# A two-layer decoder trunk on one core: accounts of written work for the scalar engine, the vector engine and SP

## The chip, the core and the metric

The kernel runs on one of the eight cores of one Trainium2 chip. The core has a tensor engine (PE, whose weight loads are shown as PEld), a vector engine (DVE), a scalar engine (ACT), GpSimd (POOL) and a sync engine (SP), which here does nothing but issue DMAs. Each engine works through its own instructions in order; semaphores hold an instruction back until its operands are there. The metric is the device time of one execution in microseconds (us), as the median of several runs. One execution more is profiled, and its trace is read below.

## The reference

Two layers on x of 512 x 2048 in float32. Each layer makes a modulated RMS norm, a branch and a gated residual add:

```python
for i in range(DEPTH):
    shift, scale, gate = jnp.split(c_act @ w_mod[i] + b_mod[i], 3, axis=-1)
    h = rms_norm(x, norm_w[i]) * (1.0 + scale) + shift
    out = fox_branch(h, ...) if i == 0 else rwkv7_branch(h, v_first, ...)
    x = x + gate * out
```

Layer 0 is a forgetting attention with 32 heads of 64. Layer 1, which the change is about, is RWKV-7 time mixing:

```python
r, k, v, z = xr @ w_in[0], xk @ w_in[1], xv @ w_in[2], xg @ w_in[3]   # x*: shifted mixes of h
kk = k * k_k;  kk = kk / max(norm(kk per head), 1e-12)
k = k * (1.0 + (a - 1.0) * k_a)
def step(S, inp):                       # 512 steps, S of 64 x 64 for each head
    S = S * w_t + (S @ a_t) b_t^T + v_t k_t^T        # a = -kk, b = kk * a
    return S, S @ r_t
y = group_norm(y) * lnx_w + lnx_b + sum(r * k * r_k) * v
return (y * silu(z)) @ w_out
```

## The kernel before

Activations are kept transposed, as 16 tiles of 128 channels by 512 tokens. Every projection is made in three passes of float32r products (weight high half x high half, low x high, high x low), so that each k step of a projection tile is three matmuls of 128x512 (`mm3`; the groups named pj<-hi,whi and so on). A weight tile of four k steps (256 KB) comes in by a DMA on SP (raw), ACT rounds it (whi, `act_hi`), and DVE subtracts (wlo). Layer 1 has 10 + 64 such tiles in one row: the rest of k, then r, v, z and at last the output projection (wo).

These projections are the **backbone** (`backbone`, L319). All else of layer 1 is done by **tasks**: Python generators that write instructions and then `yield` a distance in planned microseconds. A planned clock, `Flow.t`, goes on with each matmul that is written, by its size alone (L91 to 96). Before each k step the backbone lets every task go on whose due time has come. So the order in which instructions are written is set by those distances, and this is the order in which ACT, DVE and PE carry them out (`InOrder` chains them, and all their instructions have line L90). Where a projection's weights or operands are not written yet, the planned clock is put on by 0.2. Nothing in the plan knows how much work was already given to ACT, DVE or SP.

The tasks that the change touches, in the order of time:

- `keys` (L1305), one for each of the 16 tiles of k, started every KEY = 9.8 planned us: three loads (ip, kt, aa), a square (sq), exponentials (eI, eN), the mean of the squares by a product with a block matrix in a bank S, then kk, at, bk, their stores (atd, bkd), small products (gab) and their stores (mld). `means` (L1097) splits the square in two halves, mhi by ACT and mlo by DVE, and multiplies both into S. `mixz` makes the shifted mix for z beside it. Every four keys an inversion of small triangles is made (`invert` on POOL, for the last group on DVE; `inverse` for the products).
- `stage` (L1475), one for each of 16 units (four key tiles, two chunks of 64 tokens): loads of rt, bk, prk, then decays, and the operands of the chunk products (`products`). `bonus` makes the added term, again with `means`.
- `recur` writes the 32 steps of the recurrence, each in three hops of 3.9 planned us. `normed` (L1640) makes the group norm of a unit: two `means`, a reciprocal root, and the store ypd<-dc.
- `gated` (L1692): a tile of z goes through Silu into one of two z buffers, which frees its projection bank; when its group's ypd is complete it is loaded (yp, one buffer), multiplied (z<-z,yp) and stored (gd<-z). The output projection reads it back (hp<-gd) and splits it. The projection bank of a tile is that of the tile two before.

## Time and profile before

| | |
|---|---|
| median of 3 runs | 2400.13 us (2396.8 to 2401.81) |
| profiled execution, its own time | 2401.73 us |
| its span, first to last instruction | 2399.9 us |
| mean granted PE clock | 0.982 |
| busy share: PE, PEld, DVE, ACT, POOL | 96%, 75%, 67%, 52%, 29% |
| DMA | 480.23 MB, 200 GB/s on average |

Layer 1's backbone starts near 1179 us. The key stage runs from about 1350 to 1680 us, the recurrence to about 2190 us, and the output projection ends with the span. A row of a stage table gives the window, its length, then busy time and number of instructions of PE, PEld, DVE, ACT and POOL, the granted PE clock, the DMA share and GB/s. A row of waits says which engine and tile waited for whom, the microseconds in total, how often, and the longest. A row of a timeline has start and duration, the instruction, and in brackets the idle time of its engine just before it with what ended it.

### The profile page before, as it was taken

How to read it: one execution, taken by the hardware profiler on the slowest of the kernel's cores; microseconds unless marked ns; L12 is line 12 of the kernel's file. 1: busy time of each engine (PE TensorE's matmuls, PEld its weight loads, DVE VectorE, ACT ScalarE, POOL GpSimd, SP SyncE). 2: the span in 40 equal slices, each digit the busy share in tenths (PEclk: the TensorE clock that was granted, in tenths of full speed). 3: DMA queues.
4: the chain of work that ended last, by engine and by line, in shares of the span. 5: the costliest groups of instructions: out<-in, count | busy, mean ns of one | idle time of the engine just before them, and what ended most of it. 6: DMA issues, size and time to landing. Idle time of an engine off the chain costs nothing. (4 is left out here: it accounts for less than half of the span.)

```text
span 2399.9 us, 39413 instructions
## 1 busy us (share of the span) xinstructions
PE 2302.2 (96%) x13626; PEld 1807.3 (75%) x13626; DVE 1605.2 (67%) x2850; ACT 1256.5 (52%) x2300; POOL 694.4 (29%) x1114
## 2 busy tenths in 40 slices
PE   6999999999999999998999898899999899999999
PEld 4787777877778778886777676677777677777787
DVE  6886778888888635336797567666476776755322
ACT  4435655555565545225646777763345556665221
POOL 0002333442424210110141208771245535450000
PEclk8999999999999999999999999899999999999999
DMA  8864466766666346445756999886867766544543
GB/s 307 328 227 156 128 211 217 222 213 213 205 224 220 114 161 225 142 141 157 223 179 198 308 263 277 256 252 187 233 187 195 219 174 194 167 132 154 161 137 97
DMA packets 388152, 480.23 MB, mean 200 GB/s; under 512 B 146032, under 2 KB 217840, under 8 KB 384112
## 3 DMA queue, kind: packets, MB, share of 16 engines
q1 hardware_dynamic: 386288, 475.08, 63.7%
q0 software_dynamic: 1664, 2.63, 0.3%
q8 instruction: 108, 1.77, 0.3%
q14 instruction: 92, 0.75, 0.1%
HBM read 381.63 MB, written 95.95 MB: 199 GB/s over the span
## 5 line engine op out<-in xcount | busy, mean ns | idle before, releaser
L90 PE MATMUL pj<-hi,whi 128*128 128x512 f32 x2416 | 987.4, 409 | 11.0 <-ACT hi L90 8.2
L90 PE MATMUL pj<-hi,wlo 128*128 128x512 f32 x2416 | 959.4, 397 | 10.1 <-DVE wlo L90 10.0
L90 PE MATMUL pj<-lo,whi 128*128 128x512 f32 x2416 | 959.9, 397 | 0.0
L90 DVE TENSOR_TENSOR wlo<-raw,whi 128x512 fp32r<-128x512 f32 (+2 forms) x628 | 473.4, 761 | 255.1 <-ACT whi L90 252.4
L90 ACT ACTIVATE whi<-raw 128x512 fp32r<-128x512 f32 (+2 forms) x628 | 393.9, 634 | 399.0 <-PE pj L90 215.1
L90 PEld LDWEIGHTS pj<-hi,whi 128*128 128x128 f32 x2416 | 459.5, 190 | 116.8 <-ACT hi L90 9.2
L90 PEld LDWEIGHTS pj<-lo,whi 128*128 128x128 f32 x2416 | 458.3, 190 | 108.4 <-DVE lo L90 0.7
L90 PEld LDWEIGHTS pj<-hi,wlo 128*128 128x128 f32 x2416 | 459.9, 190 | 105.2 <-DVE wlo L90 13.4
L90 DVE CUSTOM_DVE_ANT_0 wm<-wm,cb 128x1024 f32<-128x1024 f32 x128 | 155.8, 1217 | 0.3
L90 POOL TENSOR_SCALAR SV<-SV,dec 64x64 f32<-64x64 f32 x224 | 94.2, 442 | 103.9 <-DVE SV L90 69.7
L90 ACT ACTIVATE pr<-Sm,mx 128x128 f32<-128x128 f32 (+3 forms) x128 | 71.5, 559 | 76.8 <-POOL mx L90 76.3
L90 POOL TENSOR_SCALAR pr<-pr,rc 128x128 f32<-128x128 f32 (+3 forms) x128 | 100.8, 788 | 26.0 <-DVE rc L90 23.6
L90 POOL TENSOR_SCALAR mx<-mx 128x1 f32<-128x1 f32 x128 | 59.9, 468 | 143.2 <-DVE mx L90 98.0
L90 DVE CUSTOM_DVE_ANT_0 Sm<-S,cmask 128x128 f32<-128x128 f32 (+3 forms) x128 | 62.3, 487 | 42.5 <-PE S L90 41.8
L90 POOL TENSOR_TENSOR lt<-lane 128x30 f32<-128x30 f32 (+14 forms) x90 | 64.2, 713 | 86.4 <-DMA lane<-mld 79.6
L90 POOL TENSOR_TENSOR bk<-bk,eI 128x512 f32<-128x512 f32 x32 | 36.6, 1142 | 110.3 <-PE S L90 64.0
L90 POOL TENSOR_TENSOR lane<-lane,lt 128x30 f32<-128x30 f32 (+14 forms) x90 | 64.0, 711 | 7.0
L90 PE MATMUL S<-k,q 128*128 128x128 f32 (+7 forms) x256 | 61.9, 323 | 0.0
L90 POOL TENSOR_TENSOR acc<-acc,sq 128x512 f32<-128x512 f32 x14 | 18.1, 1296 | 149.4 <-ACT sq L90 128.2
L90 ACT ACTIVATE pT<-tr 128x512 f32<-128x512 f32 x64 | 31.0, 485 | 54.4 <-PE tr L90 54.4
L90 DVE SCALAR_TENSOR_TENSOR hp<-pj,gate,hp 128x512 f32<-128x512 f32 x16 | 12.0, 751 | 68.0 <-PE pj L90 68.0
L90 PE MATMUL tr<-ident,pr 128*128 128x128 f32 x320 | 56.0, 273 | 1.5 <-DVE pT L90 1.3
(325 smaller groups left out, 3284.0 us busy)
## 6 DMA issues: line engine op xcount, KB each, us to landing
wm<-in_wmodT SPq DMA_DIRECT2D x132, 512.0 KB, 4.4
raw<-in_wz SPq DMA_DIRECT2D x128, 256.0 KB, 3.7
raw<-in_wo SPq DMA_DIRECT2D x128, 256.0 KB, 3.6
raw<-in_wv SPq DMA_DIRECT2D x124, 256.0 KB, 3.9
wm<-in_wmodT SPq DMA_DIRECT2D x30, 1024.0 KB, 6.4
raw<-in_wk SPq DMA_DIRECT2D x96, 256.0 KB, 3.7
raw<-in_wr SPq DMA_DIRECT2D x64, 256.0 KB, 5.0
raw<-in_wq SPq DMA_DIRECT2D x56, 256.0 KB, 3.5
```

The costliest lines, as they stand in the source:

```text
L90: self.last = f(*a, **k)
```

## The change

`InOrder` gets an account: `until` is the planned time at which all that was written for this engine will be done, with 0.38 for a DMA issue and 0.08 + 0.0008 for each element of a partition for other instructions (0.49 for 512). `room(left)` lets a task wait in steps of 0.2 until no more than `left` (0.6, for SP 0.8) stands open. Accounts are kept in layer 1 for ACT, DVE and SP; the backbone's own weight loads and splits are booked but do not wait, and nor do `mixing`, `mixed`, `inverse` (but for its loads), `recur`, `products`, `values` and the loads of `gathering`. The tasks above wait for room at the places that the diff shows, and at these places that are cut from it: sp.room(0.8) ahead of the stores mld<-gab and qtd<-qt and of the loads qt<-qld; in `normed` act.room() ahead of dc and of the reciprocal root, dve.room() ahead of each of the eight dc products, sp.room(0.8) ahead of ypd<-dc; dve.room() ahead of bonus's product. Some of their own distances become shorter: 8 to 6, 2.2 to 1.4 and 2 to 1.2 in `keys`; 1 to 0.4, 0.6 to nothing, 0.6 to 0.2 and 2 to 0.6 in `stage`.

```diff
     def __init__(self, tc, engine):
         self.tc, self.engine, self.on, self.last, self.clock = tc, engine, False, None, None
+        self.flow, self.until = None, 0
...
+            if self.flow and "table" not in name:
+                n = 1
+                for d in (k.get("out", a[0] if a else None)).shape[1:]:
+                    n *= d
+                self.until = max(self.until, self.flow.t) + (
+                    0.38 if name == "dma_start" else 0.08 + n * 8e-4)
             return self.last
         return issue
+
+    def room(self, left=0.6):
+
+        while self.until - self.flow.t > left:
+            yield 0.2
...
     def means(q, w, x, th, tl):
         hi = q.tile([P, T], R, tag=th, name="mhi")
         lo = q.tile([P, T], R, tag=tl, name="mlo")
+        yield from act.room()
         act_hi(hi, x)
...
         m = q.tile([P, T], F, tag="mm", name="m", bufs=2)
+        yield from act.room()
         act.activation(m, hp[:, 1:], AF.Copy, scale=omu[:, 2, k:k + 1])
         yield 1.5
+        yield from dve.room()
...
         yield 1.5
+        yield from sp.room(0.8)
         sp.dma_start(mxd[2, k], m)
...
     def keys(q, j):
         ip = q.tile([P, T], F, tag="ip", name="ip", bufs=2)
         sp.dma_start(u3(ip), of(ipd, j))
+        yield from sp.room(0.8)
         kt = load(q, kTd[j], "kt", bufs=2)
+        yield from sp.room(0.8)
         aa = load(q, aad[j], "aa", bufs=2)
-        yield 8
+        yield 6
         sq = q.tile([P, T], F, tag="sq", name="sq")
+        yield from act.room()
         act.activation(sq, kt, AF.Square, scale=col(V_KK, j))
         yield from take("eI")
         eI = eIs[0]
+        yield from act.room()
         act.activation(eI[:, :, 1:], c3(ip), AF.Exp, scale=-EDEC)
-        yield 2.2
+        yield 1.4
         ss, n = yield from means(q, blkr, sq, "mh", "ml")
...
         yield from take("eN")
+        yield from act.room()
         eN = q.tile([P, NCH, C], F, tag="eN", name="eN")
         act.activation(eN, c3(ip), AF.Exp, scale=EDEC)
-        yield 2
+        yield 1.2
...
         yield 0.7
+        yield from act.room()
         act.activation(aa, aa, AF.Identity, scale=col(V_KA, j), bias=oka[:, j:j + 1])
...
         for i in range(2):
+            yield from sp.room(0.8)
             sp.dma_start(bkd[j // NJ][:, :, i, j % NJ], ...)
...
     def stage(q, g, u):
...
-        yield 1
+        yield 0.4
         for i in range(2):
             for h in range(2):
+                yield from sp.room(0.8)
                 sp.dma_start(bk.rearrange("p j c i t -> p (j c) i t")[HS[h], :, i, :],
                              bkd[g][HS[h], u, i ^ h].rearrange("p j (c t) -> p (j c) t", c=UC))
-            yield 0.6
         yield from take("prk")
...
         yield STW
         eI = q.tile([P, NJ, UC, C], F, tag="eI", name="eI", bufs=2)
+        yield from act.room()
         act.activation(eI, prk, AF.Exp, scale=-EDEC)
         yield 1
+        yield from dve.room()
...
         for j in range(NJ):
+            yield from dve.room()
...
                 s, t = HS[h], OS[h]
+                yield from dve.room()
                 sp.dma_start(L[h][s, :, 0, :], atd[g][s, u, :, c * C:c * C + C])
...
+                yield from sp.room(0.8)
                 sp.dma_start(SV[h][t], vtd[g][(UC * u + c) * C:(UC * u + c + 1) * C, h])
...
-                yield 0.6
+                yield 0.2
             fl.start(fl.t + STW, products(q, m, c, L, SV, qp, bk, eI, dec))
-            yield 2
+            yield 0.6
...
     def bonus(q, g, u, prk):
+        yield from sp.room(0.8)
...
         sp.dma_start(u3(yp), of(ypd, j))
-        yield 4
-        yield 1
+        yield 5
+        yield from dve.room()
         dve.tensor_tensor(out=z, in0=z, in1=yp, op=OP.mult)
...
-    pe.clock = fl
+    pe.clock = act.flow = dve.flow = sp.flow = fl
```

Added lines in the class move the common line of all instructions from L90 to L91. Three places in the order of instructions follow, first before the change and then with it.

ACT in the key stage, at the fifth key: sq, eI and aa belong to it or the key before it, whi is the backbone's next weight tile, m is the mix for z, r a finished tile of r, and t the first use of the mean product.

```order
L90 ACTIVATE sq<-kt,vecs 128x512
L90 ACTIVATE eI<-ip 128x8x64
L90 ACTIVATE aa<-aa,oka,vecs 128x512
L90 ACTIVATE whi<-raw 128x512
L90 ACTIVATE m<-hp,omu 128x512
L90 ACTIVATE mhi<-sq 128x512
L90 ACTIVATE whi<-raw 128x512
L90 ACTIVATE t<-S,nfloor 128x512
```

```order
L91 ACTIVATE sq<-kt,vecs 128x512
L91 ACTIVATE eI<-ip 128x8x64
L91 ACTIVATE whi<-raw 128x512
L91 ACTIVATE aa<-aa,oka,vecs 128x512
L91 ACTIVATE mhi<-sq 128x512
L91 ACTIVATE r<-pj 128x512
L91 ACTIVATE m<-hp,omu 128x512
L91 ACTIVATE whi<-raw 128x512
L91 ACTIVATE t<-S,nfloor 128x512
```

The mix m has gone from ahead of mhi to behind it; three instructions stand between sq and mhi where four stood.

SP in the unit stage, at the loads of the tenth unit: rt, the four loads of bk and prk are the unit's, vv is its bonus's, raw is a weight tile of z.

```order
L90 DMA rt<-rTd 128x512
L90 DMA SV_20200<-vtd 64x256
L90 DMA SV_20201<-vtd 64x256
L90 DMA vvd<-vf 512x1x128
L90 DMA raw<-in_wz 128x512
L90 DMA bk<-bkd 64x8x64 x4
L90 DMA prk<-ipd 128x512
L90 DMA vv<-vvd 128x512
```

```order
L91 DMA rt<-rTd 128x512
L91 DMA raw<-in_wz 128x512
L91 DMA bk<-bkd 64x8x64 x3
L91 DMA raw<-in_wz 128x512
L91 DMA bk<-bkd 64x8x64
L91 DMA prk<-ipd 128x512
L91 DMA vv<-vvd 128x512
```

The loads of bk no longer stand in one piece; a weight load has come between them.

ACT where the output projection begins: z<-pj is the Silu of a z tile (the last two of them are tiles 14 and 15), hi<-hp and hi<-z split the output projection's operands, whi is a weight tile.

```order
L90 ACTIVATE hi<-hp 128x512 x3
L90 ACT_TABLE_LOAD
L90 ACTIVATE z<-pj 128x512
L90 ACTIVATE whi<-raw 128x512
L90 ACTIVATE hi<-hp 128x512 x2
L90 ACTIVATE whi<-raw 128x512
L90 ACTIVATE z<-pj 128x512
L90 ACTIVATE whi<-raw 128x512
L90 ACTIVATE hi<-z 128x512
```

```order
L91 ACTIVATE hi<-hp 128x512 x3
L91 ACTIVATE whi<-raw 128x512 x2
L91 ACT_TABLE_LOAD
L91 ACTIVATE z<-pj 128x512 x2
L91 ACTIVATE whi<-raw 128x512
L91 ACTIVATE hi<-hp 128x512 x2
L91 ACTIVATE whi<-raw 128x512
L91 ACTIVATE hi<-z 128x512 x2
```

The two last Silus now stand one behind the other, ahead of the weight tile and the two splits that stood between them.

More of the change, by code (lines that the diff above doesn't have):

```diff
@@ L1520, in stage @@
                                            4 * h + u, :].rearrange("j p t -> p j t"))
+                yield from sp.room(0.8)
                 sp.dma_start(SV[h][t], vtd[g][(UC * u + c) * C:(UC * u + c + 1) * C, h])
@@ L1569, in bonus @@
     def bonus(q, g, u, prk):
+        yield from sp.room(0.8)
         vv = q.tile([P, T], F, tag="vv", name="vv", bufs=1)
@@ L1659, in normed @@
         act.activation(sq, d, AF.Square)
+        yield from act.room()
         act.activation(dc, d, AF.Copy)
@@ L1668, in normed @@
             act.preload_act_table_set("natural_log_exp_and_others")
+        yield from act.room()
         r = rstd_of(q, vr, lneps, 64e-5, "sq", False, bufs=2)
@@ L1672, in normed @@
         for j in range(NJ):
+            yield from dve.room()
             s = slice(j * P, (j + 1) * P)
@@ L1676, in normed @@
         for j in range(NJ):
+            yield from dve.room()
             s = slice(j * P, (j + 1) * P)
@@ L1681, in normed @@
         yield 1.8
+        yield from sp.room(0.8)
         sp.dma_start(ypd[g][:, u], dc.rearrange("p (j t) -> p j t", j=NJ))
@@ L1704, in gated @@
         sp.dma_start(u3(yp), of(ypd, j))
-        yield 4
-        yield 1
+        yield 5
+        yield from dve.room()
         dve.tensor_tensor(out=z, in0=z, in1=yp, op=OP.mult)
```

1 line of the change is left out of this document (added).

## The prediction

> **What bounds the kernel now.** I read the page first, then busy time by stage, then what TensorE (PE) waited for in each stage, then what the engine that released it had waited for.
>
> ```profile
> span 2399.9 us, 39413 instructions
> PE 2302.2 (96%) x13626; PEld 1807.3 (75%) x13626; DVE 1605.2 (67%) x2850; ACT 1256.5 (52%) x2300; POOL 694.4 (29%) x1114
> ```
>
> PE is busy for 96% of the span, so it sets the end, and a change of order can win only PE's idle time and the time in which its clock is halved. Next the stages of layer 1's main part (time, busy time of each engine, granted clock, DMA share): the key stage, the unit stage with the recurrence, the change-over to the output projection, and the output projection.
>
> ```profile
> 1350.00:1680.00 330.00, 300.89 (x2189) 233.45 (x2188) 222.62 (x324) 213.65 (x398) 162.63 (x220) 0.93 0.86 251
> 1680.00:2190.00 510.00, 492.96 (x4696) 386.74 (x4695) 339.61 (x721) 279.44 (x485) 219.87 (x423) 0.99 0.65 182
> 2190.00:2229.00 39.00, 36.01 (x151) 27.72 (x150) 22.98 (x42) 21.93 (x35) 0.00 (x0) 1.00 0.68 215
> 2229.00:2397.00 168.00, 167.04 (x719) 135.11 (x717) 48.91 (x73) 36.03 (x57) 0.00 (x0) 1.00 0.42 129
> ```
>
> PE is idle for 29.1 us in the key stage, 17.0 in the unit stage, 3.0 in the change-over and 1.0 after it. The last row also gives PE's pace when nothing holds it: 168 / 719 = 0.234 us a matmul, 0.70 us for the three of one k step. What ended PE's waits, key stage first, then unit stage, then change-over:
>
> ```profile
> PE S L90 <- ACT mhi L90: 10.5, 5, 3.9
> PE S L90 <- DVE mlo L90: 8.4, 9, 2.0
> PE pj L90 <- DVE wlo L90: 7.1, 3, 2.8
> PE x L90 <- ACT us L90: 2.9, 4, 1.0
> ...
> PE S L90 <- ACT GP L90: 9.7, 5, 5.3
> PE S L90 <- ACT mhi L90: 3.5, 1, 3.5
> ...
> PE pj L90 <- DVE wlo L90: 2.9, 3, 1.5
> ```
>
> In the key stage 18.9 of 28.9 us is the wait of the small mean product in bank S for its operand's two halves, mhi from ACT and mlo from DVE, which `means` makes. The longest of these waits, on ACT and then on PE:
>
> ```profile
> 1554.22 0.63 ACT L90 ACTIVATE whi<-raw 128x512 fp32r<-128x512 f32 x1 [4.26 <-DMA raw<-in_wr]
> 1554.87 1.16 ACT L90 ACTIVATE qt<-x 32x256 f32<-32x256 f32 x3
> 1556.06 0.72 ACT L90 ACTIVATE sq<-kt,vecs 128x512 f32<-128x512 f32 x1
> ...
> 1558.43 0.71 ACT L90 ACTIVATE m<-hp,omu 128x512 f32<-128x512 f32 x1
> 1559.04 0.61 ACT L90 ACTIVATE mhi<-sq 128x512 fp32r<-128x512 f32 x1
> ...
> 1559.71 0.80 PE L90 MATMUL S<-mhi,blkr 128*128 128x512 f32 x1 [3.91 <-ACT mhi L90]
> ```
>
> ACT works in order. It stood 4.26 us for a weight tile that came late, and then worked off what was queued; four instructions, among them m, stood between sq and mhi (m to mhi took 0.61 us). So two things make PE late: late weight DMAs, which no account sees, and the queue ahead of mhi, which the accounts do see. The first is the larger part:
>
> ```profile
> ACT whi L90 <- DMA raw<-in_wr: 33.6, 20, 4.8
> ACT whi L90 <- DMA raw<-in_wv: 7.4, 2, 4.0
> ...
> ACT eI L90 <- DMA prk<-ipd: 7.5, 4, 4.1
> ```
>
> The first two rows are the key stage's, 41.0 us on ACT; the third is the unit stage's. Each longer wait of PE also costs clock. Windows around four mhi or mlo waits, then two of the unit stage:
>
> ```profile
> 1365.00:1380.00 15.00, 9.84 (x33) 7.34 (x32) 10.48 (x13) 13.33 (x24) 4.64 (x4) 0.77 0.88 278
> 1440.00:1455.00 15.00, 12.20 (x51) 9.03 (x50) 8.00 (x11) 10.42 (x19) 10.41 (x18) 0.77 0.98 306
> 1495.00:1505.00 10.00, 8.40 (x40) 5.85 (x39) 7.19 (x11) 7.21 (x13) 8.88 (x16) 0.83 1.07 332
> 1555.00:1567.00 12.00, 7.41 (x34) 4.95 (x33) 7.57 (x10) 9.04 (x17) 10.12 (x17) 0.72 1.04 328
> ...
> 1735.00:1745.00 10.00, 7.76 (x66) 6.08 (x68) 6.47 (x16) 4.09 (x7) 0.00 (x0) 0.83 0.72 205
> 1912.00:1925.00 13.00, 7.72 (x82) 5.80 (x82) 8.42 (x16) 7.70 (x15) 6.22 (x16) 0.74 0.85 246
> ```
>
> Length times missing clock gives 3.5 + 3.5 + 1.7 + 3.4 = 12.1 us for the four and 1.7 + 3.4 = 5.1 us for the two.
>
> **The key tasks: act.room() and sp.room().** They remove nothing and add no work; instructions change places. In the order of ACT's instructions 57 stand between the sixteen sq and their mhi before, 40 now: one fewer a key, or 0.6 us earlier by m's 0.61 us, while the planned distance from mhi to PE's product is as before. The places of SP's DMAs help less: a weight load has 4.1 others ahead of it on average both before and now, and runs of seven or more fall from nine to five. That is why I let the late DMAs stand. Taking 0.6 us off each of 5 + 9 waits gives 3.0 + 5.0 (nine of 0.93 us on average, each left with about 0.4) = 8 us. Clock falls in proportion: 8 / 18.9 of 12.1 = 5 us. Sum **−13 us**. The bounds: 0, if late DMAs set all of these waits, and −31 us, if none of them is left (18.9 + 12.1). I take the nearer to the low end because of the 41.0 us above. The waits for wlo (7.1 us) and us (2.9 us) stay. The first come where group 3's inversion runs on DVE, which stood
>
> ```profile
> 1605.52 0.19 DVE L90 TENSOR_TENSOR lt<-lane 128x30 f32<-128x30 f32 x1 [10.04 <-DMA lane<-mld]
> ```
>
> for a load that its task asks for with no distance in between; `invert` is not touched.
>
> The shorter own distances (8 to 6, 2.2 to 1.4, 2 to 1.2) I cost at nothing: the room waits ahead of them fill them up again, and the planned start of every key is the old one. Without that cover a key's three loads would be asked for about 2 us later than they are wanted, at most once a key and hidden by PE's queue of projection matmuls, until ACT stands for them; that possibility goes into the range.
>
> The Trainium skill ("TensorE: Matmul & The Clock Gate", section "Part 1: The HAM clock gate (the "warmup" mystery)") says that the clock halves after an idle window of about 3.4 us. The window at 1440 above has 2.8 us of idle in two pieces and a clock of 0.77, so here shorter waits halve it as well, and the measurement decides. By the Trainium skill's rule alone only the two longest spells would cost clock, 6.9 us instead of 12.1, and the sum would be 2 us smaller.
>
> **The unit tasks: stage, bonus, normed.** PE's 9.7 + 3.5 us come when ACT stands for prk (7.5 us) or for a weight, and the copies that free bank S stand behind it. The loads of bk ahead of prk on SP now wait for room, so prk is asked for nearer to its planned time; a weight load now stands among the four. I take a third: 13.2 / 3 = 4.4, and 0.6 of clock: **−5 us**. Bounds: 0, and −18 us (13.2 + 5.1).
>
> **The change-over pays.** The waits push the recurrence back against the projections. After the last variance product (S<-mlo,blkr) PE has 858 projection matmuls left before and 822 now; the last 768 are the output's. So the output's first tile starts 90 x 0.234 = 21.1 us after it before, and 54 x 0.234 = 12.6 us now: 8.4 us of cover is gone. What has to happen between, as it ran before:
>
> ```profile
> 2192.96 0.69 ACT L90 ACTIVATE sq<-S,lneps 128x512 f32<-128x512 f32 x1
> 2197.69 0.33 SPq L90 DMA_DIRECT2D ypd<-dc  x1
> 2199.92 0.52 SPq L90 DMA_DIRECT2D yp<-ypd  x1
> 2204.45 0.69 DVE L90 TENSOR_TENSOR z<-z,yp 128x512 f32<-128x512 f32 x1 [1.14 <-DMA yp<-ypd]
> 2205.17 0.52 SPq L90 DMA_DIRECT2D yp<-ypd  x1
> 2206.41 1.36 SPq L90 DMA_DIRECT2D gd<-z  x1
> 2208.99 0.69 DVE L90 TENSOR_TENSOR z<-z,yp 128x512 f32<-128x512 f32 x1 [3.85 <-DMA yp<-ypd]
> 2211.68 0.60 ACT L90 ACTIVATE z<-pj 128x512 f32<-128x512 f32 x1
> ```
>
> The Silu of tile 14 frees the bank of the output's first tile, and it writes the z buffer that the store of tile 12 (gd<-z) reads. Counted from the first row, that store is issued at +13.5; with 2.2 us to land (the store of ypd, 2197.69, to the load that waits for it, 2199.92) and 0.6 for the Silu the bank is free at +16.3. Before, this was 4.8 us early; now it is 3.7 us late. The Silu of tile 15 stands right behind on ACT and waits for the second product (+16.0), which is 0.4 us later than its own tile wants; the weight halves that queue behind these two cost an estimated 1.5 us, the length of the longest wlo wait here. A PE wait of that length cost 3.4 us of clock at 1555. The 2.9 us of wlo waits there now go under. 3.7 + 0.4 + 1.5 + 3.4 − 2.9 = **+6 us**. Bounds: 0 if the bank comes in time, and +12 (8.4 + 3.4).
>
> **Sum.** The profiled execution took 2401.73 us, 1.6 above the median of the runs: 2401.7 − 13 − 5 + 6 = 2389.7, and at the median **2388 us**. Its own range, with half and one and a half of the gain of 18 and the cost between 3 and 9: 2376 to 2400.
>
> **Rivals.** First, **nothing to gain**: the key stage is held by the DMA engines, whose share is 0.86 on average and 0.98 to 1.07 in three of the four windows above, so the weights come late in any order. Against it: the window at 1365 has 0.88, and the average leaves 14%. Then 0 to −6 us there and in the units against +6: 2400. The Trainium skill ("DMA: Bandwidth & Descriptors", section "Specifications") asks for 512 B or more in a transfer for line rate; that speaks for this rival and is a limit that order does not move. The row
>
> ```profile
> DMA packets 110265, 82.68 MB, mean 251 GB/s; under 512 B 41531, under 2 KB 84027, under 8 KB 110233
> ```
>
> of this stage shows 38% of packets below that. By that rule alone the time would stay at 2400.
>
> Second, **slower by the change-over**: the chain above is serial over one yp buffer, ACT stands in order with both Silus ahead of the weights, and so the whole 8.4 us comes back as PE idle, with 3.4 of clock; where the gain upstream is under 4 us, the time is above 2405, at 2409 with none (2400.1 + 8.4 + 3.4 − 2.9). It decides as soon as the store of tile 12 lands after the last projection of tile 15. Against it: part of the 8.4 us was slack (4.8 us).
>
> Third, **most S waits vanish**: half a microsecond was often all that lacked (mean mlo wait 0.93 us), and one avoided wait spares the clock for the next key. Three quarters of 31 + 18 against +6: 2401.7 − 37 + 6 − 1.6 = 2369.
>
> **Chances.** Forecast 0.42, nothing to gain 0.20, slower by the change-over 0.22, most S waits vanish 0.16. What a measurement here can tell from no change is about 0.2%, 4.8 us: faster means under 2395.3. Of the forecast's 0.42 I count 0.38 there and 0.04 as the same; of the first rival 0.03 falls below. Faster 0.57, same 0.21, slower 0.22. Cases of both signs count, so the range for 8 in 10 goes from the third rival to the second: 2367 to 2408.
>
> **What would show it.** Right: PE's mhi and mlo waits in the key stage fall from 18.9 to about 11 us while ACT's waits for raw stay near 41; PE's waits for GP fall in the unit stage; a new wait of pj for ACT z, near 4 us, stands at the start of the output projection. Wrong: raw waits fall as well (then SP's places matter more than I count, and the third rival is near); no wait for ACT z (the change-over was covered); new ACT waits for kt or aa (the short distances were too short); or mhi waits as long as before with the clock again at 0.93.

## The result, and the profile after

| | before | after |
|---|---|---|
| median | 2400.97 us (2396.8 to 2408.12, 4 runs) | 2425.3 us (2423.27 to 2429.01, 4 runs) |
| ratio, 95% interval | | 1.0099, 1.0083 to 1.0116 |
| profiled execution's span | 2399.9 us | 2424.3 us |

The change makes the kernel 1.0% slower, 24 us. The prediction was 2388 us, faster; sign and range were both wrong. First the page of after:

```profile
span 2424.3 us, 39413 instructions
PE 2313.8 (95%) x13626; PEld 1814.1 (75%) x13626; DVE 1614.3 (67%) x2850; ACT 1261.3 (52%) x2303; POOL 700.4 (29%) x1114
```

PE's work is the same, ACT has three table loads more (35 for 32), and PE is still the engine that sets the end. Next the stage tables of both kernels, this time cut at events instead of fixed times, so that they can be compared: layer 1's backbone up to the first unit, the unit stage with the recurrence up to the last variance product, and the change-over with the output projection. Before:

```profile
1179.00:1709.00 530.00, 493.74 (x3120) 381.01 (x3119) 368.69 (x504) 326.80 (x601) 211.39 (x270) 0.96 0.80 239
1709.00:2192.00 483.00, 465.96 (x4458) 364.84 (x4457) 329.47 (x704) 269.90 (x466) 215.11 (x406) 0.99 0.64 177
2192.00:2400.00 208.00, 201.05 (x860) 161.22 (x858) 70.89 (x113) 56.51 (x90) 0.00 (x0) 1.00 0.47 145
```

After:

```profile
1182.00:1719.00 537.00, 497.39 (x3145) 383.74 (x3144) 367.60 (x506) 326.61 (x601) 211.71 (x270) 0.97 0.80 238
1719.00:2219.00 500.00, 475.55 (x4468) 369.82 (x4467) 343.93 (x710) 279.57 (x476) 219.31 (x406) 0.98 0.62 172
2219.00:2424.00 205.00, 194.78 (x825) 156.74 (x823) 66.37 (x106) 51.86 (x82) 0.00 (x0) 0.98 0.46 140
```

Projection matmuls move between the stages with the order, so a stage's length isn't its loss. What can be compared is PE's idle time (the exact length less PE's busy time) plus the clock it lost (half of the time for which the trace's clock records give half speed). The change-over is counted to PE's last matmul. "Key stage" is the first row. "Cover" is the number of projection matmuls that PE still has ahead of the output projection when the last variance product is done:

| us idle + lost clock | layer 0 | key stage | unit stage | change-over and output | cover (matmuls) | median us |
|---|---|---|---|---|---|---|
| before | 52.9 | 58.5 | 22.1 | 3.0 | 90 | 2401 |
| after | 53.1 | 55.0 | 34.6 | 11.6 | 54 | 2425 |
| difference | +0.2 | −3.5 | **+12.5** | **+8.6** | | +24 |

The sum is 17.8 us of 24.4. Of the rest, 2.7 us lie in layer 0, where PE's order is the same in both kernels; across the profiles below layer 0 took between 1177.0 and 1184.2 us. So a few us in one profile carry nothing. The measure of the table scatters too: in layer 0, where the order is one in all the profiles below, it runs from 47.3 to 56.9 us, and e4 below, whose order is that of the kernel before until 1700 us, has 53.2 us in its key stage for 58.5. The remaining 4 us I can't place.

PE's waits after, first in the key stage (1350 to 1680 us):

```profile
PE S L91 <- DVE mlo L91: 9.7, 10, 3.0
PE S L91 <- ACT mhi L91: 9.5, 8, 2.0
PE pj L91 <- DVE wlo L91: 8.7, 3, 5.0
PE S L91 <- ACT gab L91: 2.6, 1, 2.6
```

mhi and mlo together are 19.2 us, 18.9 before: nothing was won. In the unit stage (1680 to 2190 us), before (the rows that the prediction doesn't show) and after:

```profile
PE S L90 <- DVE mlo L90: 1.8, 4, 0.6
...
PE S L90 <- DVE vf L90: 0.3, 1, 0.3
```

```profile
PE S L91 <- ACT GP L91: 6.7, 4, 3.4
PE S L91 <- DVE mlo L91: 5.6, 7, 2.2
PE S L91 <- ACT mhi L91: 3.2, 1, 3.2
PE S L91 <- ACT sq L91: 2.5, 2, 1.4
PE S L91 <- POOL SV L91: 1.7, 1, 1.7
PE S L91 <- DVE vf L91: 1.7, 1, 1.7
```

The waits for prk, from which the prediction started here, went as it said:

```profile
ACT eI L91 <- DMA prk<-ipd: 1.6, 2, 0.9
```

They took 7.5 us before. GP fell from 9.7 to 6.7 us, but mlo rose from 1.8 to 5.6 and vf from 0.3 to 1.7, and sq and POOL's SV are new. What ACT itself waited for in the key stage:

```profile
ACT whi L91 <- DMA raw<-in_wr: 40.8, 23, 4.8
...
ACT whi L91 <- DMA raw<-in_wv: 7.2, 5, 2.2
```

and, before and then after, in the unit stage:

```profile
ACT whi L90 <- DMA raw<-in_wv: 23.8, 13, 5.2
```

```profile
ACT whi L91 <- DMA raw<-in_wv: 31.7, 11, 5.7
```

ACT's waits for late weights rose from 41.0 to 48.0 and from 23.8 to 31.7 us. Why a shorter queue ahead of mhi did not shorten PE's waits is seen at a key of after, on ACT, PE and DVE:

```profile
1508.28 0.63 ACT L91 ACTIVATE whi<-raw 128x512 fp32r<-128x512 f32 x1 [4.36 <-DMA raw<-in_wr]
1508.82 0.71 ACT L91 ACTIVATE sq<-kt,vecs 128x512 f32<-128x512 f32 x1
...
1510.65 0.61 ACT L91 ACTIVATE mhi<-sq 128x512 fp32r<-128x512 f32 x1
...
1511.32 0.50 PE L91 MATMUL S<-mhi,blkr 128*128 128x512 f32 x1 [1.51 <-ACT mhi L91]
...
1512.39 1.06 DVE L91 TENSOR_TENSOR mlo<-sq,mhi 128x512 fp32r<-128x512 f32 x1
...
1513.51 0.50 PE L91 MATMUL S<-mlo,blkr 128*128 128x512 f32 x1 [1.69 <-DVE mlo L91]
```

ACT stood 4.36 us for a weight tile ahead of sq, and though only eI and aa stand between sq and mhi, PE still waited. All five of PE's mhi waits before (10.5 us) have such a stall of ACT, 1.8 to 4.3 us long, ahead of sq. Of the eight after the change (9.5 us), three (5.4 us) are of this kind; three (1.8 us) have a weight stall of 1.5 to 2.2 us between sq and mhi; and in two (2.3 us) ACT stood there 2.1 and 2.7 us with eI, for DVE to write at. Over the sixteen keys ACT ran 57 instructions between sq and mhi before and 40 after, nine of them whi in both; the idle time ahead of those nine rose from 1.5 to 11.0 us, and the mean time from the start of sq to that of mhi from 2.91 to 3.21 us.

At the change-over, on ACT and then on PE:

```profile
2220.78 0.69 ACT L91 ACTIVATE sq<-S,lneps 128x512 f32<-128x512 f32 x1
...
2236.61 1.28 ACT L91 ACT_TABLE_LOAD   x1 [5.63 <-DVE z L91]
2237.90 0.60 ACT L91 ACTIVATE z<-pj 128x512 f32<-128x512 f32 x1
...
2238.55 0.80 PE L91 MATMUL pj<-hi,whi 128*128 128x512 f32 x1 [6.45 <-ACT z L91]
```

```profile
2230.00:2245.00 15.00, 8.55 (x25) 6.45 (x25) 3.67 (x6) 4.83 (x8) 0.00 (x0) 0.66 0.71 218
```

The predicted new wait is there, 6.45 us long, with 15 x 0.34 = 5.1 us of clock behind it.

### The profile page after: what moved, and what is told of

Read it like the earlier page. It is cut to its first block, busy times and chain, and to the rows that moved or that the text cites. A ratio compares the mean times of both kernels' runs of the same rounds, so it can differ in the third digit from the quotient of the medians.

```text
span 2424.3 us, 39413 instructions
## 1 busy us (share of the span) xinstructions
PE 2313.8 (95%) x13626; PEld 1814.1 (75%) x13626; DVE 1614.3 (67%) x2850; ACT 1261.3 (52%) x2303; POOL 700.4 (29%) x1114
## 5 line engine op out<-in xcount | busy, mean ns | idle before, releaser
L91 PE MATMUL pj<-hi,whi 128*128 128x512 f32 x2416 | 991.9, 411 | 17.8 <-ACT hi L91 8.2
L91 PE MATMUL pj<-hi,wlo 128*128 128x512 f32 x2416 | 962.4, 398 | 8.7 <-DVE wlo L91 8.7
L91 PE MATMUL pj<-lo,whi 128*128 128x512 f32 x2416 | 962.5, 398 | 0.0
L91 DVE TENSOR_TENSOR wlo<-raw,whi 128x512 fp32r<-128x512 f32 (+2 forms) x628 | 467.8, 752 | 273.1 <-ACT whi L91 270.6
L91 ACT ACTIVATE whi<-raw 128x512 fp32r<-128x512 f32 (+2 forms) x628 | 394.2, 634 | 415.9 <-PE pj L91 231.8
L91 PEld LDWEIGHTS pj<-hi,whi 128*128 128x128 f32 x2416 | 461.5, 191 | 124.5 <-ACT hi L91 9.0
L91 PEld LDWEIGHTS pj<-lo,whi 128*128 128x128 f32 x2416 | 460.3, 191 | 109.1 <-DVE lo L91 0.2
L91 PEld LDWEIGHTS pj<-hi,wlo 128*128 128x128 f32 x2416 | 462.0, 191 | 102.9 <-DVE wlo L91 10.7
L91 DVE CUSTOM_DVE_ANT_0 wm<-wm,cb 128x1024 f32<-128x1024 f32 x128 | 155.7, 1216 | 0.3
L91 POOL TENSOR_SCALAR SV<-SV,dec 64x64 f32<-64x64 f32 x224 | 94.3, 443 | 90.8 <-DVE SV L91 77.6
L91 ACT ACTIVATE pr<-Sm,mx 128x128 f32<-128x128 f32 (+3 forms) x128 | 71.5, 559 | 77.0 <-POOL mx L91 76.4
L91 POOL TENSOR_SCALAR pr<-pr,rc 128x128 f32<-128x128 f32 (+3 forms) x128 | 101.3, 791 | 25.8 <-DVE rc L91 23.6
L91 POOL TENSOR_SCALAR mx<-mx 128x1 f32<-128x1 f32 x128 | 60.0, 469 | 145.3 <-DVE mx L91 100.3
L91 DVE CUSTOM_DVE_ANT_0 Sm<-S,cmask 128x128 f32<-128x128 f32 (+3 forms) x128 | 62.2, 486 | 42.5 <-PE S L91 41.9
L91 POOL TENSOR_TENSOR lt<-lane 128x30 f32<-128x30 f32 (+14 forms) x90 | 62.5, 695 | 84.6 <-DMA lane<-mld 77.7
L91 POOL TENSOR_TENSOR bk<-bk,eI 128x512 f32<-128x512 f32 x32 | 38.0, 1189 | 125.3 <-PE S L91 73.3
L91 POOL TENSOR_TENSOR lane<-lane,lt 128x30 f32<-128x30 f32 (+14 forms) x90 | 65.3, 725 | 7.1
L91 PE MATMUL S<-k,q 128*128 128x128 f32 (+7 forms) x256 | 61.9, 323 | 0.0
L91 POOL TENSOR_TENSOR acc<-acc,sq 128x512 f32<-128x512 f32 x14 | 18.2, 1297 | 149.0 <-ACT sq L91 149.0
L91 ACT ACTIVATE pT<-tr 128x512 f32<-128x512 f32 x64 | 31.1, 486 | 54.4 <-PE tr L91 54.4
L91 PE MATMUL tr<-ident,pr 128*128 128x128 f32 x320 | 56.0, 273 | 1.5 <-DVE pT L91 1.3
L91 DVE SCALAR_TENSOR_TENSOR hp<-pj,gate,hp 128x512 f32<-128x512 f32 x16 | 12.0, 750 | 68.2 <-PE pj L91 68.2
```

The lines of the kernel that those rows point to most:

```text
L91: self.last = f(*a, **k)
```

## The experiments

All ratios are against the kernel before on the same chip. The theories at the start were: **Theory 1**, each part of the change has its own price; **Theory 2**, the schedule's constants fit the old order, and any order that moves loses.

**The parts alone, and a shift that has nothing to do with the change.** e1 keeps the waits for room in `keys`, `mixz`, `inverse` and `means` with keys' shorter distances, and undoes the rest:

```diff
     def stage(q, g, u):
-        yield 0.4
+        yield 1
...
-                yield from sp.room(0.8)
```

(likewise all of stage, bonus, normed and gated).

> The change's key part alone (keys, mixz, inverse, and the wait in means); stage, bonus, normed and gated as before. 54 projection matmuls of cover stay behind the last variance product, as with the whole change (90 before). Theory 1, each part has its own price (key part about -4 us, change-over +9 wherever the cover is 54, unit part +12): about 2405 us, with a PE wait of 5 to 7 us for ACT z at the first output tile, and PE idle of about 17 us in the unit stage as before. Theory 2, the constants of the schedule fit the old order, and any order that moves the unit stage against the projections loses: 2412 to 2422 us, with 22 us or more idle in the unit stage although its tasks are the old ones.

Measured 2418.89 us, ratio 1.0085 (1.0055 to 1.0115). e2 is the other half: `stage`, `bonus`, `normed`, `gated` and `means` as changed, and undone

```diff
     def keys(q, j):
-        yield from sp.room(0.8)
...
-        yield 6
+        yield 8
```

with all of mixz and inverse.

> The change's unit part alone (stage, bonus, normed, gated, and the wait in means); keys, mixz and inverse as before. 90 matmuls of cover, as before. Theory 1: no wait for ACT z at the first output tile; unit part +12: about 2412 us. Theory 2: about the same, 2408 to 2420. If the unit part costs nothing (2398 to 2404), the whole loss comes from the later start of the recurrence that the key part brings.

Measured 2437.4 us, 1.0159 (1.0129 to 1.019). e3 has all the shorter distances and no `yield from ….room()` at all.

> All shorter distances, no task waits for room (the accounts are kept and never asked). 72 matmuls of cover. Theory 1: the waits for room are what pushes products and stores back; without them the unit stage is as before or better and the change-over costs 18 matmuls x 0.234 = 4 us less 4.8 us of slack, about nothing: 2398 to 2404 us. Theory 2: 2408 to 2420 us, since the order is a new one again.

Measured 2456.28 us, 1.0231 (1.0202 to 1.026). e4 is the kernel before with a constant of the unit stage moved:

```diff
-    STW = 5
+    STW = 5.4
```

> The kernel before with one constant moved: STW, the planned distance from a unit's last load to its first use, 5.4 for 5. No account, no wait for room. 72 matmuls of cover instead of 90. Theory 1: 2398 to 2404 us (slack of 4.8 us covers the 18 matmuls; one distance is longer and loads are in time more often). Theory 2: a moved order loses whatever moved it: 2408 to 2420 us, with 20 us or more of PE idle in the unit stage.

Measured 2421.0 us, 1.0088 (1.0059 to 1.0116). By stage:

| us idle + lost clock | key | unit | change-over, output | cover | median |
|---|---|---|---|---|---|
| before | 58.5 | 22.1 | 3.0 | 90 | 2400 |
| e1 keys alone | 60.0 | 22.0 | 15.0 | 54 | 2419 |
| e2 units alone | 69.7 | 44.6 | 3.8 | 90 | 2437 |
| e3 distances alone | 55.0 | 70.5 | 9.3 | 72 | 2456 |
| e4 STW 5.4 | 53.2 | 33.6 | 11.3 | 72 | 2421 |

The parts don't add up: 19 + 37 against 24 for both. e2 and e3 came out above both theories' ranges, e4 1 us above Theory 2's. The change-over follows the cover, as Theory 1 says (3 to 4 us at 90, 9 to 11 at 72, 12 to 15 at 54). e1 has the time of Theory 2, but its unit stage, with the unit tasks as they were, lost no more than before (22.0 us, with PE idle for 20.3 us, between the 17 of Theory 1 and the 22 of Theory 2), while e2, with the new unit tasks alone, lost 44.6 us there. So the unit tasks' own waits for room stay a suspect. But e4, which holds no line of the change, loses as much as the change does, and 11.5 us of it in the unit stage, where the change lost 12.5. The waits for room, on the other hand, hold something together: the short distances without them lost 48 us more in the unit stage than the kernel before. There PE waited, in e3,

```profile
PE S L91 <- DVE mlo L91: 32.5, 18, 10.1
PE S L91 <- ACT GP L91: 15.7, 7, 9.3
```

**What can be done about the change-over.** e5 gives the last two Silus another buffer:

```diff
-        yield from take("z")
-        z = mq.tile([P, T], F, tag="z", name="z")
+        late = j >= KT - 2
+        yield from take("m" if late else "z")
+        if late:
+            z = mq.tile([P, T], F, tag="hp", name="zl", bufs=NHP)
+        else:
+            z = mq.tile([P, T], F, tag="z", name="z")
...
-        free["z"] += 1
+        if not late:
+            free["z"] += 1
...
+            free["m"] += 1
```

> The changed kernel, but z of tiles 14 and 15 is written into a buffer of the ring hp (five buffers) instead of the ring z (two), so the Silu of tile 14 no longer waits for the product and the store of tile 12. Nothing else in the schedule moves; 54 projection matmuls lie behind the last variance product as in the changed kernel. Theory 1 (the change-over costs because the bank of the output's first tile is freed late, through that z buffer): the wait pj <- ACT z of 6.45 us and the 10.2 us at half clock behind it (5.1 us) are gone, about 1 to 3 us of wlo waits come back: 2414 to 2418 us. Theory 2 (the products and stores themselves are late, and the output's last two k steps wait for them in another place): 2422 to 2427, with a new wait of pj for hi or lo of tile 14 or 15 of the gated activations.

Measured 2424.66 us, 1.0098 (1.0081 to 1.0114); no gain. The wait on ACT z is gone and another stands in its place. PE's waits in e5 from the last variance product to 2260 us, and then ACT's:

```profile
PE pj L91 <- ACT whi L91: 4.1, 1, 4.1
PE pj L91 <- DVE wlo L91: 2.7, 2, 2.0
```

```profile
ACT hi L91 <- DMA hp<-gd: 11.9, 2, 9.0
```

ACT, in order, now stood 9.0 us for a gated tile that had to be stored and read back, with a weight half behind it. The buffer was only the first thing in a chain that is late as a whole. The time is that of the second theory, though PE's new wait is for a weight's halves and not for hi or lo of tile 14 or 15, as it said.

e6 gives `stage` its old distances and keeps every wait for room:

```diff
-        yield 0.4
+        yield 1
...
+            yield 0.6
...
-                yield 0.2
+                yield 0.6
...
-            yield 0.6
+            yield 2
```

> The changed kernel with stage's own distances as before (1, 0.6, 0.6, 2 us) and all room waits kept. No projection matmul (0) lies behind the last variance product ahead of the output's; 54 in the changed kernel, 90 before. Theory 1 (each part has its own price): the change-over waits 54 x 0.234 = 12.6 us longer than in the changed kernel, some 19 us in all with 5 us of clock, and the unit stage, which lost 12 us through the shorter distances, is back at 22 us of idle time and lost clock: about 2426. Theory 2 (the schedule's constants fit the old order, and any moved order loses in the unit stage): the unit stage stays at 33 us or more, about 2438 or above.

Measured 2428.33 us, 1.011 (1.0087 to 1.0134). The time is near Theory 1's 2426 and 10 us below Theory 2's, but the unit stage stays at 34.1 us, as Theory 2 says, so beside the waits for room the shorter distances cost nothing that this run can tell. The cover is 0, and the change-over and output lost 24.6 us. PE's wait there, and the clock around it:

```profile
PE pj L91 <- ACT z L91: 15.4, 1, 15.4
```

```profile
2224.00:2246.00 22.00, 5.69 (x14) 3.90 (x15) 4.86 (x12) 5.42 (x9) 0.00 (x0) 0.53 0.36 118
```

From 54 to 0 matmuls of cover the wait grew by 15.4 − 6.45 = 8.9 us where 12.6 were expected. In the other direction, e12 below, with a cover of 126, lost 0.4 us there. Over all the profiles this wait for ACT z sorts by the cover: none in the nine with 90 or more, 5.3 to 6.7 us in the four with 72, 6.45 to 7.1 in the five with 54 (e5 apart), 15.4 with none. So cover decides whether the wait is there, but not at a fixed price: the 18 matmuls (4.2 us) from 72 to 54 cost about 1 us.

**How much any shift costs.** Two more shifts of the kernel before, with its cover of 90 kept:

```diff
-    INV, KEY = 54, 9.8
+    INV, KEY = 55, 9.8      (e7)
+    INV, KEY = 54, 9.7      (e8)
```

> The kernel before with INV = 55 for 54: the first inverse task of a group starts 1 us later in the plan. No room wait, no distance changed; cover at the change-over 90 as before. Theory 1 (what costs is the parts of the change and the cover): 2398 to 2404, unit stage at 22 us of idle time and lost clock. Theory 2 (the constants were fitted to this one order; any order that moves loses): 2408 to 2420, with 28 to 40 us in the unit stage, and nothing at the change-over.

> The kernel before with KEY = 9.7 for 9.8: a key task starts 0.1 us sooner after the one before it, so the sixteenth starts 1.5 us earlier in the plan. Cover at the change-over 90 as before. Theory 1: 2397 to 2405 (key stage within 3 us, unit stage at 22 us of idle time and lost clock). Theory 2: 2408 to 2420, in the key stage and the unit stage together.

e7 took 2412.29 us, 1.0049 (1.0034 to 1.0065); e8 2417.4 us, 1.0067 (1.0052 to 1.0082). Their unit stages lost 27.9 and 31.4 us, their change-overs 4.7 and 3.9. Theory 1's numbers are excluded for these two. The same two shifts, and one of the recurrence's step, made in the changed kernel:

```diff
-    INV, KEY = 54, 9.8
+    INV, KEY = 55, 9.8      (e10)
+    INV, KEY = 54, 9.7      (e11)
-    HOP = 3.9
+    HOP = 3.7               (e12)
```

> The changed kernel with INV = 55 for 54, the same shift that cost the kernel before 11 us. Cover 54 as in the changed kernel. Theory 1 (the change has a price of its own, in the unit tasks and at the change-over): 2425 plus about 11, 2430 to 2440. Theory 2 (the kernel before is one fitted point, and a shift loses from there and from nowhere else): 2415 to 2430, the unit stage between 25 and 40 us of idle time and lost clock, the change-over as in the changed kernel.

> The changed kernel with KEY = 9.7 for 9.8, the same shift that cost the kernel before 16 us. Cover 54. Theory 1: 2425 plus about 16, 2433 to 2445. Theory 2: 2415 to 2430, as the changed kernel within the scatter of the three shifts of the kernel before (11, 16 and 21 us).

> The changed kernel with HOP = 3.7 for 3.9: the planned distance between two steps of the recurrence is 0.2 us shorter, so the recurrence ends earlier against the projections, with 126 projection matmuls behind the last variance product (54 in the changed kernel, 90 before). Theory 1: the change-over costs nothing (idle time and lost clock of the change-over and the output near 3 us for 11.6), the unit stage keeps its 12 us: 2414 to 2419. Theory 2: the change-over costs nothing, the unit stage moves at random between 25 and 50 us: 2408 to 2435. If the shorter steps come too early for their operands, waits of x and y for SV appear on PE, over 10 us in all: above 2430.

| median us | as it is | INV 55 | KEY 9.7 | STW 5.4 | HOP 3.7 |
|---|---|---|---|---|---|
| kernel before | 2401 | 2412 | 2417 | 2421 | – |
| changed kernel | 2425 | 2431 (1.0112, 1.0087 to 1.0138) | 2411 (1.0036, 1.0026 to 1.0046) | – | 2412 (1.005, 1.0034 to 1.0066) |

The kernel before loses under each of its three shifts (mean 2417); the changed kernel gains 14 and 13 us under two and loses 6 under one (mean of the four 2420). KEY 9.7 costs the one kernel 16 us and gives the other 14. So the kernel before stands on an order that is better than these three neighbours, and the changed kernel is one of many; e9 below shows that one neighbour is better still. STW 5.4 in the changed kernel and HOP 3.7 in the kernel before were not run. e10 (2431) lies inside Theory 1's range and 1 us above Theory 2's; its runs, 2424 to 2434, reach into both, so it speaks a little for Theory 1. e11 (2411) is below both, on Theory 2's side, with a unit stage of 22.9 us, as good as before's. e12 (2412) is in Theory 2's range and just below Theory 1's; its change-over was free, as both said. Its unit stage lost 29.8 us.

**What is better about the one order: late weight loads.** In the plan a weight tile is halved 4.5 us behind its load. How long the load takes from issue to landing stands in the list of DMA issues, here of the kernel before in the key stage (the last number is the median):

```profile
raw<-in_wr SPq DMA_DIRECT2D x64, 256.0 KB, 5.0
```

More than half of these loads take longer than 4.5 us. A planned us is somewhat longer than a measured one, since the plan counts a matmul of this size at 512 / 2400 = 0.213 us and PE needs 0.234; so not every such load is late, but ACT stood 20 times for them in this stage. e9 is the kernel before with

```diff
         def fetch(n):
...
-            yield 4.5
+            yield 6 if lead == 14 else 4.5      (lead is 14 in layer 1 alone)
```

> The kernel before, but in layer 1 the halving of a weight tile (whi on ACT, wlo on DVE) stands 6.0 us behind its load in the plan for 4.5. No load is asked for at another time by this edit itself; the cover at the change-over stays 90 matmuls. Theory A (late weight loads set the key stage's waits: ACT stands for raw, and mhi and mlo are late behind it): ACT's waits for raw in the key stage fall from 41 us to under 15, PE's waits for mhi and mlo from 18.9 to under 8, with 6 us of clock: 2380 to 2392. Theory B (those waits come from the queue of ACT and DVE, and a stall for raw only hides idle time that would come anyway): raw waits fall, mhi and mlo stay at 15 us or more, and the time is 2400 to 2415.

Measured **2390.45 us, 0.9958 (0.9938 to 0.9977)**: faster than both kernels. Its stages (the windows of the prediction):

```profile
1350.00:1680.00 330.00, 303.18 (x2279) 234.40 (x2277) 220.60 (x329) 214.21 (x401) 162.14 (x220) 0.96 0.87 256
1680.00:2190.00 510.00, 498.68 (x4678) 391.69 (x4671) 346.82 (x735) 286.13 (x497) 223.97 (x423) 0.99 0.66 183
```

ACT's waits for weights in the key stage, and PE's waits there:

```profile
ACT whi L90 <- DMA raw<-in_wr: 12.2, 9, 2.3
ACT whi L90 <- DMA raw<-in_wv: 2.2, 2, 1.3
```

```profile
PE pj L90 <- DVE wlo L90: 10.1, 7, 4.5
PE S L90 <- ACT mhi L90: 7.0, 3, 2.5
PE S L90 <- DVE mlo L90: 5.0, 7, 2.0
```

The raw waits fell from 41.0 to 14.4 us as Theory A says, and mhi and mlo from 18.9 to 12.0, where it named under 8. The time from sq to mhi meanwhile grew to 3.72 us, so it is not this distance that sets PE's waits; wlo, now made later, rose from 7.1 to 10.1. Idle time and lost clock came to 49.2 us in the key stage (58.5 before) and 12.8 in the unit stage (22.1). This profile is of the fastest of the six runs (2386 us), and 5 us of its gain lie in layer 0, where nothing differs; the 11 us are the medians' difference. The DMA share of the key stage is 0.87 where it was 0.86, so full DMA engines were not what held the kernel before.

The same edit in the changed kernel (e13), in it with KEY 9.7 (e14), in it with HOP 3.7 (e15), and with 7.0 in the kernel before (e16):

> The changed kernel with the halving of a weight tile 6.0 us behind its load in layer 1 (4.5 in the changed kernel); 72 projection matmuls of cover. If late weight loads are what the changed kernel loses in its unit stage (ACT's waits for raw there 23.8 us before, 31.7 with the change), those fall under 18 us, the unit stage's idle time and lost clock fall from 34.6 to 15 to 22, the key stage's from 55 to 45 to 50, the change-over keeps 6 to 9: 2400 to 2408, as far below the changed kernel as 6.0 took the kernel before (11 us) or further. If the loss in the unit stage is the price of the room waits or of the reshuffle, the unit stage stays above 28 and the time at 2413 to 2425.

> The changed kernel with KEY = 9.7 and the halving 6.0 us behind its load; 72 matmuls of cover. With KEY = 9.7 alone it took 2411. If late loads are the cause: 2392 to 2402. If not: 2408 to 2420.

> The changed kernel with HOP = 3.7 and the halving 6.0 us behind its load; 162 matmuls of cover, so nothing at the change-over. With HOP = 3.7 alone it took 2412. If late loads are the cause: 2388 to 2400, with the unit stage between 15 and 25 us. If not: 2408 to 2420.

> The kernel before with the halving 7.0 us behind its load; cover 90. If the raw waits that 6.0 us left (14.4 us in the key stage, 14.8 in the unit stage) still hold PE: raw waits under 5 us in each stage and 2380 to 2390. If what is left at 6.0 us comes from elsewhere, or the halves now come late for PE itself: 2388 to 2405, with PE's waits for wlo above the 10 us that 6.0 left in the key stage.

| halving behind the load | 4.5 us | 6.0 us | 7.0 us |
|---|---|---|---|
| kernel before | 2401 | 2390 (e9) | 2405 (e16: 1.0012, 1.0001 to 1.0023) |
| changed kernel | 2425 | 2409 (e13: 1.0035, 1.0024 to 1.0047) | – |
| changed, KEY 9.7 | 2411 | 2412 (e14: 1.0044, 1.0029 to 1.0059) | – |
| changed, HOP 3.7 | 2412 | 2404 (e15: 1.0008, 0.9998 to 1.0018) | – |

The edit of e16 is `yield 7` where e9 has `yield 6`; that of the others is e9's line. e13 won back 17 us of the 24 and ended 0.6 us above its first range. ACT in its unit stage:

```profile
ACT whi L91 <- DMA raw<-in_wv: 17.0, 8, 5.5
```

The raw wait is about half of the changed kernel's 31.7, and idle time with lost clock 27.3 us for 34.6, where 15 to 22 was expected: part of the unit stage's loss is late loads, not all. Its change-over, expected at 6 to 9 us, lost 13.5. e14 gained nothing, against its first expectation; e15 gained 8 and ended 4 above its range. Over the four pairs the 6.0 us gained 11, 17, −1 and 8 us, about 9 on average, so this gain is not one lucky order alone. e16 shows the other end of the scale. Its waits in the key stage:

```profile
ACT whi L90 <- DMA raw<-in_wr: 2.0, 4, 1.3
```

```profile
PE pj L90 <- DVE wlo L90: 16.8, 9, 6.6
```

ACT hardly waits there any more (in the unit stage it still waits 14.9 us for weights), and PE waits for the halves themselves, as the second expectation of e16 has it.

**The store that waits for room.** In e2's trace one wait stood out: the vector engine's last instruction on a unit's result, the store of it on SP, and the scalar engine's next use of that buffer:

```profile
1920.34 0.34 DVE L91 SCALAR_TENSOR_TENSOR dc<-dc,vecs,bv 128x128 f32<-128x128 f32 x1
...
1932.79 0.43 SPq L91 DMA_DIRECT2D ypd<-dc  x1
...
1937.56 0.60 ACT L91 ACTIVATE ys<-y 128x512 f32<-128x512 f32 x1 [18.52 <-DMA ypd<-dc]
```

The result was ready at 1920.7 us; its store went out 12 us later, behind loads for other units, and ACT stood 18.5 us, since ys of the next unit takes the buffer that the store reads. e17 takes the one line out of e2, e18 out of the changed kernel:

```diff
-        yield from sp.room(0.8)
         sp.dma_start(ypd[g][:, u], dc.rearrange("p (j t) -> p j t", j=NJ))
```

> The kernel of e2_units_alone (2437 us) without the one sp.room(0.8) ahead of normed's store ypd<-dc. In e2 ACT stood 18.5 us at 1937 us for that store, since ys of the next unit is written into the one buffer that the store reads, and PE then waited 14.4 us for mhi with 17.1 us at half clock. If the room wait ahead of the store made it late: ACT's waits of ys for ypd<-dc fall from 26.7 us to under 8, the 14.4 us wait is gone, and the time is 2410 to 2420. If the store was late for another reason (the SP queue as such, the variance chain): the long wait stays, 2430 to 2440.

> The changed kernel without the one sp.room(0.8) ahead of normed's store ypd<-dc. ACT's waits of ys for that store were 11.2 us (longest 5.5), and one of PE's longest waits of the unit stage (3.25 us at 1811 us, with 6.8 us at half clock) stands behind one of 4.9 us. If that room wait is part of the unit stage's loss: ys waits under 5 us and 2415 to 2421. If it only mattered in e2's order: 2422 to 2430.

e17 took 2430.48 us, 1.0121 (1.0103 to 1.0139), 7 below e2, though the two intervals overlap; that is the second theory's range by half a us. Its longest wait of this kind:

```profile
1924.40 0.60 ACT L91 ACTIVATE ys<-y 128x512 f32<-128x512 f32 x1 [9.12 <-DMA ypd<-dc]
```

The wait for room made that store later, but half of the stall stays without it. e18 took 2423.11 us, 1.0088 (1.0067 to 1.011), which can't be told from the changed kernel, and its ys waits did not fall (16.9 us for 11.2). So this line may matter in e2's order, and in the change's nothing shows that it does.

## Why the prediction was wrong

**What bounds the kernel** held: PE sets the end, its waits are short and come mostly in S, the longer ones cost clock, and ACT's stalls for weights are ahead of them.

**The key tasks, −13 us: this step failed.** It took 0.6 us off each of fourteen waits because fewer instructions stand between sq and mhi. They are fewer (40 for 57), but mhi and mlo took 19.2 us in all (18.9 before), and with lost clock the stage won 3.5 us, less than the scatter between profiles. This is the prediction's own lower bound, "0, if late DMAs set all of these waits": more than half of the mhi waits (5.4 of 9.5 us) follow, as all of them did before, a stall of ACT for a weight tile ahead of sq, which a shorter queue behind sq does not take away, and more of the stalls for weights now fall between sq and mhi (11.0 us, 1.5 before). e9 confirms it from the other side: later halving took the waits to 12.0 us although the distance from sq to mhi grew. The prediction had named the late weight loads as the larger part and then "let them stand"; they rose by 7 us, and moving the halves behind them was worth 11 us in the kernel before.

**The shorter own distances, at nothing** held with the waits for room: ACT's waits for kt took 0.5 us. Without them (e3) ACT stood 7.9 us for kt, as the prediction feared, but the key stage lost 55.0 us as in the changed kernel. What the prediction left without a price are the shorter distances of `stage`: with the waits for room they cost nothing that can be told (e6 against the changed kernel: unit stage 34.1 and 34.6 us), without them e3's unit stage lost 48 us more than the kernel before.

**The unit tasks, −5 us: this step failed by its sign.** The mechanism it named worked: ACT's waits for prk fell from 7.5 to 1.6 us and PE's wait for GP by a third, 9.7 to 6.7 us. Around it mlo rose by 3.8 us, sq, SV and more of vf came, ACT's raw waits rose by 7.9 us, and the stage lost 12.5 us in all. The error is to have priced one named wait and to have taken the rest of a moved order as unchanged. Three shifts of the kernel before raise the same stage by 5.8, 9.3 and 11.5 us without any line of the change, so the 12.5 us are no measure of what the waits for room cost as such. Nor are they cleared: e1, without the new unit tasks, lost no more there than the kernel before.

**The change-over, +6 us** had the right mechanism and was too small: 8.6 us measured, inside its bounds of 0 to 12. The wait for ACT z was 6.45 us where 4 were named, and the clock lost 5.1 us where 3.4 were. The difference lies mostly in two table loads of 1.28 us. One stands ahead of the Silu, so the bank was free 17.7 us behind the chain's first row (2220.78 to 2238.50) and not 16.3. Another put that first row 1.3 us behind the end of the variance product (0.6 before), from which the 12.6 us of cover count. The "4.8 us early" were not all there either: at a cover of 72, which takes 4.2 us away, four kernels waited 5.3 to 6.7 us.

**The rivals.** "Slower by the change-over" (2409) named the right place for a third of the loss, and nearly its size (8.4 + 3.4 − 2.9 = 8.9 us for 8.6); its condition came true, as the store of tile 12 was issued at 2233.39, after PE's last projection matmul at 2231.70. "Nothing to gain", with full DMA engines, had the right outcome for the key stage by the wrong cause: e9 won 11 us with the same transfers, at a share of 0.87. The rival that was missing is that the order before was fitted: three shifts without any line of the change lose 11 to 21 us, so a change that moves everything may lose as much before its own merits count. That this is what happened to the unit stage is argued from the shifts and not shown; the later halving, a shift too, gained.

**Open** is what the unit stage's loss consists of beyond late weight loads, and whether the waits for room cost or are worth anything on an order that is fitted to them. The four orders of the changed kernel average 2420 us and the three shifted ones of the kernel before 2417; with so few, that tells no difference.

## What to carry to other kernels

In a schedule planned by constants, compare a change with shifted copies of the kernel before, not with the kernel before alone: here three small shifts, of one constant each, cost 11, 16 and 21 us, nearly as much as the whole change (24). An in-order engine that stands for a late transfer makes everything behind it late, so price the stall and what stands behind it before the queue's length, and compare the planned distance from load to use with the measured landing (4.5 us against 5.0 here; 6.0 gave 11 us, 7.0 gave nothing). A wait put ahead of a store can delay whoever writes that buffer next.

## What the runs showed of the hardware

The clock stays low longer than the wait that lowers it. In e6, with a wait of 15.4 us, the granted clock over 22 us was 0.53: 22 x 0.47 x 2 = 20.7 us at half speed. In the changed kernel 6.45 us of waiting brought 15 x 0.34 x 2 = 10.2 us. A single short wait can be enough:

```profile
2004.28 1.16 PE L91 MATMUL S<-L,bk 64*128 64x128 f32 x14 [1.39 <-ACT sq L91]
```

In the 6.8 us ahead of 2005.5 PE had no other idle time than these 1.39 us, and there the clock records of the changed kernel give 3.4 us at half speed. In the clock records of all these profiles the spells at half speed inside the kernel are 3.4, 6.8, 10.2, 13.7, 17.1 or 20.5 us long, that is whole multiples of 3.4 us. The Trainium skill ("TensorE: Matmul & The Clock Gate", section "Part 1: The HAM clock gate (the "warmup" mystery)") gives about 3.4 us as the idle window; the length of the spells agrees with that number, while a wait shorter than it, the 1.39 us above, lowered the clock as well.
